# A two-block transformer on one core: the order of each engine from a simulated timeline

## The chip, the cores and the metric

The kernel runs on one core of one Trainium2 chip. The metric is the device time of the run in microseconds (us), as the median of three runs. The core's engines are TensorE (PE; its weight loads are listed as PEld), VectorE (DVE), ScalarE (ACT), GpSimd (POOL) and SyncE (SP), which here issues the DMAs of the weights. Each works off its own queue of instructions, in the order that was fixed when the program was built; they wait for one another by semaphores.

## The reference

256 tokens of width 1024 go through a first block of two layers (gated linear attention, GLA, then stick-breaking attention, SB; each followed by a squared-ReLU MLP, and each addition by a layer norm) and a second block of two layers (forgetting attention and retention side by side, a gated convolutional feed-forward net, a gated per-layer embedding), with a final rms norm. Cut to what matters here:

```python
def first_block(x, ...):
    for layer in range(DEPTH):                 # layer 0: GLA, layer 1: stick-breaking
        mix = gla_mixer(h, ...) if layer < N_A else stick_breaking_attention(q, k_sh, v_sh) @ sb_w_o[j]
        h = layer_norm(DEEPNORM_ALPHA * h + mix, ln_g[layer, 0], ln_b[layer, 0])
        h = layer_norm(DEEPNORM_ALPHA * h + sq_relu_mlp(h, mlp_w_up[layer], mlp_w_down[layer]),
                       ln_g[layer, 1], ln_b[layer, 1])

def gla_mixer(x, w_in, w_a2, b_a, norm_g, w_o):
    proj = x @ w_in                            # q, k, v, g and the low-rank gate a1
    o = gla_chunked(q, k, v, log_a)
    o = o * lax.rsqrt(jnp.mean(jnp.square(o), axis=-1, keepdims=True) + RMS_EPS) * norm_g
    return (o * jax.nn.silu(g)) @ w_o

def sq_relu_mlp(x, w_up, w_down):
    h = jax.nn.relu(x @ w_up)
    return (h * h) @ w_down
```

## The kernel before

All activations stay on the chip, features on the partitions and the 256 tokens along the row. What takes the time is the weights: some 220 MB of float32 are streamed from HBM once, in the order of the list `STREAM`. `prep` (L325 to L333) issues the DMA of half a block of weights into `raw` (128x1024, four buffers), casts it on ACT to `wh` (L330), and subtracts on DVE to get the remainder `wl` (L333); six buffers of each. Activations are split the same way by `split` (cast L467 on ACT, subtraction L468 on DVE). Every product is then three matmuls in `mm3`: wh·xh (L402), wh·xl (L403), wl·xh (L404), 128 columns of weights against 256 tokens, or 512 columns where a projection is kept with tokens on the partitions (`proj_tok`).

PSUM holds four `acc` tiles, three `up` tiles and one `aux` tile; a fourth projection into `up` has to wait until the first has been read.

At a layer norm, `layer_norm` centres the sum on an estimate of the mean and gives the un-normed, scaled input `xg`. `early` multiplies the first weight blocks of what comes next with it (matmuls of 128x258, two columns more for gain and bias). In the middle of these, `stats` sums x and its squares over the features by four fp32 matmuls (L586), L588 to L592 form mean and variance, `rsqrt` takes Ln and Exp on ACT and three steps on DVE (L501 to L503), and L597 subtracts the mean. `normed` multiplies by the reciprocal root (L618), applies gain and bias on ACT (L622) and splits (L467, L468); `settle` (L665 to L667) corrects the early products afterwards, and the MLP squares its ReLU in L712. In the second block `normed` also multiplies by an rms weight and has its own steps (L624, L626, L627, L644).

The GLA layer takes its rms norm by column sums into `aux` (L530), gates with Silu from `up` tiles (L396, behind a load of ACT's function table, L390). Stick-breaking and forgetting attention take scores (L916, L920; L1119, L1120) and multiply the weights with the values (L979, L981) into `aux`, which `split` reads for the output projection. These attention stages are called from hooks between the steps of the projections, so in program order they lie between matmuls that don't need them.

The program's order is not the order of the engines. The Tile framework gives each instruction a priority, `tc.cur_priority`, that grows along the program; `prep` adds `LATER` = 150 to that of the casts and subtractions of weights. When the context closes, a scheduler goes through the instructions and lays each engine's queue out by what is ready when, and by priority. What it takes for "ready when" is the subject of the change. Dependences without a semaphore (`add_manual_dep`) are added in a few places, as for weight casts that must not come before the end of a norm (`self.after`, the last step of `rsqrt`).

Of the kernel before, what the change touches and what calls it, by code (L numbers as in the profile page):

```python
# [1413 lines left out]
@with_exitstack  # L1414
def program(ctx: ExitStack, tc: tile.TileContext, A, out, stop=None):
    Net(ctx, tc, A, out, stop).run()


def build(inputs, stop=None):
    import concourse.bacc as bacc  # L1420

    nc = bacc.Bacc("TRN2", target_bir_lowering=False, num_devices=1)
    host, aps = {}, {}
    for name, a in arrays(inputs).items():
        host[f"in_{name}_dram"] = a
        aps[name] = nc.dram_tensor(f"in_{name}_dram", a.shape, mybir.dt.from_np(a.dtype), kind="ExternalInput").ap()
    out = nc.dram_tensor("out_0_dram", (T, D), F32, kind="ExternalOutput").ap()
    with tile.TileContext(nc) as tc:
        program(tc, aps, out, stop)
    return nc, host  # L1430

# [8 lines left out]
```

## Time and profile before

| | |
|---|---|
| time, median of 3 runs | 1300.72 us (1300.63 to 1301.56) |
| the profiled execution: its own time | 1304.21 us |
| its span | 1302.4 us |
| busy: PE, DVE, ACT | 1283.7, 950.8, 754.4 us |
| read from HBM | 227.96 MB, 177 GB/s over the span |
| mean granted clock of PE | 0.997 |

The span is the stretch of the profiled execution from the first to the last instruction. Busy time is the union of an engine's instructions, and matmuls overlap in it, so it can't be divided by their number; the distance between their starts is what one costs. "Idle before" an instruction, with the releaser behind the arrow, is a wait. Granted clock 1.00 is the upper of PE's two levels (2.4 GHz), 0.50 the lower (1.2 GHz).

### The profile page before, as it was taken

To read this page: it belongs to the slowest core of one execution; us is meant where nothing else is said; L and a number is where in the kernel's file an instruction comes from. 1 tells how busy PE (TensorE), PEld (TensorE's weight loads), DVE (VectorE), ACT (ScalarE), POOL (GpSimd) and SP (SyncE) were. 2 spreads that over 40 slices of the span, in tenths; PEclk is the share of its full clock that TensorE was granted. 3 is DMA by queue.
4 is the path that set the end of the run, shared out by engine and by line. 5 is a ranking of instruction groups with operands and counts; after the bars stand their busy time and mean duration, and the time that the engine had idled before them with its cause. 6 is when DMAs were issued, how large, how long until landed. Compare 5 with 4: busy or idle time off the path is not lost.

```text
span 1302.4 us, 25441 instructions
## 1 busy us (share of the span) xinstructions
PE 1283.7 (99%) x10302; PEld 1235.9 (95%) x10302; DVE 950.8 (73%) x1526; ACT 754.4 (58%) x1194; POOL 37.2 (3%) x89
## 2 busy tenths in 40 slices
PE   8999999999999999999999999999999999999997
PEld 6999999999899999999989999999999899999996
DVE  6989955559657955558878788765787869885855
ACT  6566744447786754446746665544674557554544
POOL 0000000000231000000000000000001000000000
PEclk9999999999999999999999999999999999999999
DMA  8655666654533576555664466565647446666561
GB/s 278 226 165 161 195 191 182 186 180 141 186 118 114 170 230 189 183 190 196 206 195 135 143 202 188 181 186 155 217 155 228 145 129 196 189 184 188 173 218 54
DMA packets 64694, 232.78 MB, mean 179 GB/s; under 512 B 7216, under 2 KB 7488, under 8 KB 63936
## 3 DMA queue, kind: packets, MB, share of 16 engines
q1 hardware_dynamic: 61920, 220.75, 54.0%
q10 hardware_dynamic: 2016, 8.28, 1.7%
q0 software_dynamic: 640, 2.11, 0.5%
q8 instruction: 81, 1.33, 0.4%
q14 instruction: 37, 0.30, 0.1%
HBM read 227.96 MB, written 3.16 MB: 177 GB/s over the span
## 4 chain that ended last, share of the span: by engine, by line
PE 88%; DVE 5%; DMA 3%; ACT 2%; issue 1%; POOL 0%; SPq 0%; POOLq 0%; DVEq 0%; ACTq 0%
PE up L402 19%; PE up L403 19%; PE up L404 19%; PE acc L403 9%; PE acc L404 8%; PE acc L402 8%; DVE wl L333 2%; DMA raw<-in_w_pg_dram 1%; PE aux L979 1%; ACT wh L330 1%; DMA wa<-in_w_a_dram 1%; PE acc L1130 1%; PE aux L586 1%; DMA raw<-in_w_gv_dram 0%; PE acc L1073 0%
## 5 line engine op out<-in xcount | busy, mean ns | idle before, releaser
L333 DVE TENSOR_TENSOR wl<-raw,wh 128x1024 fp32r<-128x1024 f32 (+2 forms) x420 | 505.3, 1207 | 257.8 <-ACT wh L330 256.2
L330 ACT CAST wh<-raw 128x1024 fp32r<-128x1024 f32 (+2 forms) x420 | 434.5, 1036 | 384.3 <-PE acc L403 141.3
L402 PE MATMUL up<-b,wh 128*128 128x256 f32 (+1 forms) x2032 | 575.0, 283 | 3.1 <-DVE pleg L1268 1.8
L403 PE MATMUL up<-b,wh 128*128 128x256 f32 (+1 forms) x2032 | 573.2, 282 | 0.9 <-DVE b L515 0.8
L404 PE MATMUL up<-b,wl 128*128 128x256 f32 (+1 forms) x2032 | 570.6, 281 | 0.0
L402 PEld LDWEIGHTS up<-b,wh 128*128 128x128 f32 x2032 | 382.2, 188 | 8.8 <-issue 3.4
L403 PEld LDWEIGHTS up<-b,wh 128*128 128x128 f32 x2032 | 383.4, 189 | 3.7 <-issue 1.6
L404 PEld LDWEIGHTS up<-b,wl 128*128 128x128 f32 x2032 | 383.6, 189 | 0.9 <-issue 0.8
L403 PE MATMUL acc<-b,wh 128*128 128x256 f32 (+1 forms) x960 | 270.6, 282 | 0.0
L404 PE MATMUL acc<-b,wl 128*128 128x256 f32 (+1 forms) x960 | 270.4, 282 | 0.0
L402 PE MATMUL acc<-b,wh 128*128 128x256 f32 (+1 forms) x960 | 270.2, 281 | 0.0
L402 PEld LDWEIGHTS acc<-b,wh 128*128 128x128 f32 x960 | 181.1, 189 | 0.1
L403 PEld LDWEIGHTS acc<-b,wh 128*128 128x128 f32 x960 | 181.0, 189 | 0.1
L404 PEld LDWEIGHTS acc<-b,wl 128*128 128x128 f32 x960 | 180.7, 188 | 0.1
L402 PE MATMUL up<-wh,b 128*128 128x512 f32 (+1 forms) x136 | 52.5, 390 | 1.6 <-ACT wh L361 1.6
L403 PE MATMUL up<-wl,b 128*128 128x512 f32 (+1 forms) x136 | 51.9, 382 | 0.0
L404 PE MATMUL up<-wh,b 128*128 128x512 f32 (+1 forms) x136 | 51.6, 381 | 0.0
L467 ACT CAST b<-ffny 128x256 fp32r<-128x256 f32 x44 | 17.9, 407 | 54.4 <-DVE ffny L1204 52.1
L402 PEld LDWEIGHTS up<-wh,b 128*128 128x128 f32 x136 | 25.5, 188 | 8.3 <-ACT wh L361 2.3
L404 PEld LDWEIGHTS up<-wh,b 128*128 128x128 f32 x136 | 25.5, 188 | 5.3
L403 PEld LDWEIGHTS up<-wl,b 128*128 128x128 f32 x136 | 25.6, 188 | 4.9 <-DVE wl L362 0.4
L1196 DVE TENSOR_TENSOR glaS<-up,rfr 128x256 f32<-128x256 f32 x44 | 18.7, 425 | 12.4 <-PE up L404 12.3
(266 smaller groups left out, 1166.2 us busy)
## 6 DMA issues: line engine op xcount, KB each, us to landing
raw<-in_w_fu_dram SPq DMA_DIRECT2D x88, 512.0 KB, 4.4
raw<-in_w_mu_dram SPq DMA_DIRECT2D x64, 512.0 KB, 4.3
raw<-in_w_md_dram SPq DMA_DIRECT2D x64, 512.0 KB, 4.6
raw<-in_w_fd_dram SPq DMA_DIRECT2D x32, 512.0 KB, 4.4
raw<-in_w_sqk_dram SPq DMA_DIRECT2D x16, 512.0 KB, 4.4
raw<-in_w_rqk_dram SPq DMA_DIRECT2D x16, 512.0 KB, 4.8
raw<-in_w_fqk_dram SPq DMA_DIRECT2D x16, 512.0 KB, 4.0
raw<-in_w_out_dram SPq DMA_DIRECT2D x16, 512.0 KB, 4.0
```

Of the source, the lines that this page charges most:

```text
L330: i = nc.scalar.copy(hi, r).ins
L333: i = nc.vector.tensor_tensor(out=lo, in0=r, in1=hi, op=ALU.subtract).ins
L402: mm(o, wh, xh, start=first, stop=False, skip_group_check=True)
L403: mm(o, wh, xl, start=False, stop=False, skip_group_check=True)
L404: self.last_mm = mm(o, wl, xh, start=False, stop=last, skip_group_check=True).ins
L467: nc.scalar.copy(out[0][:, i, :], src)
L586: nc.tensor.matmul(ps[:, k, :], ones, s[k][:, i, :], start=(k == 0 and i == 0), stop=(i == 1), skip_group_check=True)
L979: self.nc.tensor.matmul(pO[r, i // 2, :], v[:, 0, hc], ws[i][:, 0:256], start=(i < 2), stop=False, skip_group_check=True)
L1130: mm(pls[i][:, a:b], qk[r, 0, a:a + P], qk[r, 1, 0:b - a], start=(a == 0), stop=True, skip_group_check=True)
L1196: nc.vector.tensor_tensor(out=a[:, 2:], in0=ps[:, 0, :], in1=R, op=ALU.mult)
```

## The change

```diff
-    with tile.TileContext(nc) as tc:
+    with tile.TileContext(nc, schedule_with_timeline_sim=True) as tc:
         program(tc, aps, out, stop)
```

One argument is given to the context (L1428): the order of the instructions on each engine is laid out on a timeline that is simulated, in place of an estimate. Instructions, tiles, buffers and priorities in the code are the same: 10003 matmuls, the same DMAs in the same order on SP's queue. The rows of PE's order differ in 2424 lines of some 9900, DVE's in 1664 of some 1470 rows (both sides counted), ACT's in 1248 of some 1130, POOL's in 11. The orders of the two programs follow, at the places of which the prediction speaks.

PE in the GLA layer before: aux_152 is the norm's column sum, its second matmul the one that ends it; up_151 is the second block of the gate weights w_gg.

```order
L404 MATMUL up_151_872<-b8_4_88,wl_93_557 128x256
L530 MATMUL aux_152_897<-sumh_143_849,one_148 128x256
L402 MATMUL up_151_872<-b8_4_88,wh_95_562 128x256
L403 MATMUL up_151_872<-b8_5_89,wh_95_562 128x256
L404 MATMUL up_151_872<-b8_4_88,wl_96_563 128x256
L530 MATMUL aux_152_897<-suml_144_850,one_148 128x256
L402 MATMUL up_151_872<-b8_4_88,wh_95_562 128x256
```

PE there in the changed program: up_164 is the third block, up_172 the fourth, which takes the `up` slot of the first.

```order
L403 MATMUL up_164_959<-b8_5_89,wh_113_663 128x256
L530 MATMUL aux_152_897<-suml_144_850,one_148 128x256
L404 MATMUL up_164_959<-b8_4_88,wl_114_664 128x256
L402 MATMUL up_164_959<-b8_4_88,wh_113_663 128x256
L403 MATMUL up_164_959<-b8_5_89,wh_113_663 128x256
L404 MATMUL up_164_959<-b8_4_88,wl_114_664 128x256
L402 MATMUL up_172_1026<-b8_4_88,wh_128_761 128x256
```

The end of the column sum moved from the second block to the last matmuls of the third, four ahead of up_172.

PE at the entry of the first MLP before: aux_223 are the sums of x (lnsum_177) and of its squares (lnsum_178); acc_215 and acc_216 are early products of the first block of w_mu, which is at its start here.

```order
L402 MATMUL acc_216_1380<-b8_175_1082,wh_190_1147 128x258
L403 MATMUL acc_216_1380<-b8_176_1083,wh_190_1147 128x258
L404 MATMUL acc_216_1380<-b8_175_1082,wl_191_1148 128x258
L586 MATMUL aux_223_1429<-lnsum_177_1088,tab0_82 128x256 x2
L586 MATMUL aux_223_1429<-lnsum_178_1089,tab0_82 128x256 x2
L402 MATMUL acc_215_1379<-b8_175_1082,wh_190_1147 128x258
L403 MATMUL acc_215_1379<-b8_176_1083,wh_190_1147 128x258
```

PE there in the changed program; acc_229 is an early product of the second block, up_237 of the third.

```order
L402 MATMUL up_237_1527<-b8_175_1082,wh_207_1309 128x258
L403 MATMUL up_237_1527<-b8_176_1083,wh_207_1309 128x258
L586 MATMUL aux_223_1429<-lnsum_177_1088,tab0_82 128x256 x2
L403 MATMUL acc_215_1379<-b8_176_1083,wh_190_1147 128x258
...
L404 MATMUL acc_215_1379<-b8_175_1082,wl_191_1148 128x258
L402 MATMUL acc_216_1380<-b8_175_1082,wh_190_1147 128x258
L403 MATMUL acc_216_1380<-b8_176_1083,wh_190_1147 128x258
L586 MATMUL aux_223_1429<-lnsum_178_1089,tab0_82 128x256 x2
L404 MATMUL acc_216_1380<-b8_175_1082,wl_191_1148 128x258
L403 MATMUL acc_229_1465<-b8_176_1083,wh_201_1243 128x258
```

The sums stood together among the first block's early products, 108 matmuls ahead of the first one on the normed x (up_273); now early products of all three blocks stand ahead of them, the sum of the squares comes eight matmuls after the sum of x, and 51 matmuls ahead of up_273. (The second MLP's entry has the same pattern: 107 before, 30 now, with 16 matmuls between the two sums.)

DVE at the entry of the first MLP before, from the end of the reciprocal root (rfr_228, L503) to the first split of the normed x (b8_247): lnq is the normed x before gain and bias, erz the correction of early products.

```order
L503 SCALAR_TENSOR_TENSOR rfr_228_1442<-rfa_227_1441,rfr_228_1442 128x256
L666 SCALAR_TENSOR_TENSOR erz_256_1620<-spread_224_1434,erk_255_1619,acc_215_1379 128x256
L618 TENSOR_TENSOR lnq_248_1592<-b8_174_1081,rfr_228_1442 128x512
L618 TENSOR_TENSOR lnq_249_1598<-b8_174_1081,rfr_228_1442 128x512
L666 SCALAR_TENSOR_TENSOR erz_256_1620<-spread_224_1434,erk_255_1619,acc_216_1380 128x256
L666 SCALAR_TENSOR_TENSOR erz_260_1634<-spread_224_1434,erk_259_1633,acc_229_1465 128x256
L667 TENSOR_TENSOR erz_256_1620<-erz_256_1620,rfr_228_1442 128x512
L618 TENSOR_TENSOR lnq_250_1604<-b8_174_1081,rfr_228_1442 128x512
L333 TENSOR_TENSOR wl_233_1470<-raw_231_1467,wh_232_1469 128x1024
L468 TENSOR_TENSOR b8_247_1591<-b8_245_1589,b8_246_1590 128x512
```

DVE there in the changed program, from the second lnq on; lnq_248, all four L666 and the four L597 stand ahead of these rows.

```order
L618 TENSOR_TENSOR lnq_249_1598<-b8_174_1081,rfr_228_1442 128x512
L667 TENSOR_TENSOR erz_256_1620<-erz_256_1620,rfr_228_1442 128x512
L667 TENSOR_TENSOR erz_260_1634<-erz_260_1634,rfr_228_1442 128x512
L333 TENSOR_TENSOR wl_233_1470<-raw_231_1467,wh_232_1469 128x1024
L333 TENSOR_TENSOR wl_236_1476<-raw_234_1473,wh_235_1475 128x1024
L333 TENSOR_TENSOR wl_241_1532<-raw_239_1529,wh_240_1531 128x1024
L333 TENSOR_TENSOR wl_244_1538<-raw_242_1535,wh_243_1537 128x1024
L618 TENSOR_TENSOR lnq_250_1604<-b8_174_1081,rfr_228_1442 128x512
L618 TENSOR_TENSOR lnq_251_1610<-b8_174_1081,rfr_228_1442 128x512
L712 TENSOR_TENSOR relu2_257_1628<-relu_254_1618 128x512
L712 TENSOR_TENSOR relu2_261_1642<-relu_258_1632 128x512
L468 TENSOR_TENSOR b8_247_1591<-b8_245_1589,b8_246_1590 128x512 x2
```

One weight subtraction (L333) and three lnq stood between; now it is four subtractions, all four lnq and two squares of the MLP (L712), which need the early products.

PE at the entry of the stick-breaking layer before: up_525 is an early product, up_554 and up_555 the value projection (first matmuls on the normed x), acc_568 and acc_569 the first scores.

```order
L402 MATMUL up_525_3703<-b8_466_3262,wh_498_3492 128x258
L403 MATMUL up_525_3703<-b8_467_3263,wh_498_3492 128x258
L404 MATMUL up_525_3703<-b8_466_3262,wl_499_3493 128x258
L402 MATMUL up_554_3830<-wh_505_3559,b8_533_3765 128x512
L403 MATMUL up_554_3830<-wl_506_3560,b8_533_3765 128x512
...
L404 MATMUL up_555_3831<-wh_519_3644,b8_534_3766 128x512
L916 MATMUL acc_568_3889<-qk_541_3798 128x256
L916 MATMUL acc_569_3891<-qk_541_3798 128x256
L920 MATMUL acc_568_3889<-qk_541_3798 128x128
L920 MATMUL acc_569_3891<-qk_541_3798 128x128
```

PE there in the changed program; acc_594 and acc_595 are the scores of the second pair of heads.

```order
L404 MATMUL up_525_3703<-b8_466_3262,wl_499_3493 128x258
L916 MATMUL acc_568_3889<-qk_541_3798 128x256
L916 MATMUL acc_569_3891<-qk_541_3798 128x256
L920 MATMUL acc_568_3889<-qk_541_3798 128x128
L920 MATMUL acc_569_3891<-qk_541_3798 128x128
L916 MATMUL acc_594_4005<-qk_545_3810 128x256
L916 MATMUL acc_595_4007<-qk_545_3810 128x256
L920 MATMUL acc_594_4005<-qk_545_3810 128x128
L920 MATMUL acc_595_4007<-qk_545_3810 128x128
L402 MATMUL up_554_3830<-wh_505_3559,b8_533_3765 128x512
```

The scores of two pairs of heads stand in front of the value projection, where those of one stood 33 matmuls behind its start.

At the ends of the attentions (the L981 matmul into `aux`, then the split) the output projection's matmuls that read the split result now follow directly: once at w_so (up_717) and three times at w_out (up_1308, up_1911 twice); 36 matmuls or more stood between. At the second block's entry the four sums stand 26 instead of 48 matmuls ahead of the first one on the normed x.

## Rows read from the trace of the kernel before

**Rows 1.** The page: busy us (share of the span) and instructions of each engine

```profile
PE 1283.7 (99%) x10302; PEld 1235.9 (95%) x10302; DVE 950.8 (73%) x1526; ACT 754.4 (58%) x1194; POOL 37.2 (3%) x89
```

**Rows 2.** Waits of PE: waiting tile and line, releaser, sum us, times, longest

```profile
PE up L402 <- DVE pleg L1268: 1.8, 1, 1.8
PE acc L764 <- DVE wl L333: 1.7, 1, 1.7
PE up L402 <- ACT wh L361: 1.6, 1, 1.6
...
PE up L402 <- ACT b L626: 1.2, 1, 1.2
PE up L403 <- DVE b L515: 0.8, 2, 0.5
PE acc L830 <- DVE glaQ L823: 0.4, 1, 0.4
PE acc L937 <- ACT sbh L931: 0.4, 1, 0.4
PE aux L586 <- DVE lnsum L578: 0.3, 1, 0.3
```

**Rows 3.** Windows: stretch, us, busy us of five engines, PE clock, DMA share, GB/s

```profile
120.00:280.00 160.00, 160.00 (x1350) 159.92 (x1349) 101.16 (x118) 83.83 (x115) 0.00 (x0) 1.00 0.61 188
608.61:614.18 5.57, 5.57 (x26) 4.32 (x24) 5.25 (x13) 3.57 (x7) 0.00 (x0) 1.00 0.65 218
951.40:953.50 2.10, 0.31 (x3) 0.11 (x1) 2.10 (x6) 1.08 (x2) 0.00 (x0) 1.00 0.00 0
954.44:957.85 3.41, 3.41 (x18) 3.41 (x17) 2.31 (x7) 1.91 (x5) 0.00 (x0) 0.50 0.52 159
957.85:961.26 3.41, 3.41 (x31) 3.41 (x30) 3.06 (x7) 3.16 (x4) 0.00 (x0) 1.00 0.00 0
20.40:24.40 4.00, 3.89 (x20) 3.21 (x21) 4.00 (x7) 4.00 (x9) 0.00 (x0) 1.00 0.62 173
```

**Rows 4.** ACT's timeline at the GLA gates: start us, us, instruction

```profile
76.59 1.05 ACT L330 CAST wh<-raw 128x1024 fp32r<-128x1024 f32 x1 [1.49 <-PE up L403]
77.76 0.42 ACT L396 ACTIVATE rfa<-rfv 128x256 f32<-128x256 f32 x1
78.21 0.42 ACT L396 ACTIVATE rfr<-rfa 128x256 f32<-128x256 f32 x1
78.64 1.28 ACT L390 ACT_TABLE_LOAD   x1
79.94 1.09 ACT L396 ACTIVATE glaG<-up 128x512 f32<-128x512 f32 x2
```

**Rows 5.** Timelines of ACT (one row) and DVE at the first MLP's entry

```profile
120.75 0.39 ACT L588 ACTIVATE spread<-aux 128x256 f32<-128x256 f32 x1 [2.21 <-PE aux L586]
...
125.25 1.22 DVE L333 TENSOR_TENSOR wl<-raw,wh 128x1024 fp32r<-128x1024 f32 x1
126.39 0.42 DVE L503 SCALAR_TENSOR_TENSOR rfr<-rfa,rfr 128x256 f32<-128x256 f32 x1
126.72 0.47 DVE L666 SCALAR_TENSOR_TENSOR erz<-spread,erk,acc 128x256 f32<-128x256 f32 x1
127.11 1.29 DVE L618 TENSOR_TENSOR lnq<-b,rfr 128x512 f32<-128x512 f32 x2
128.32 0.86 DVE L666 SCALAR_TENSOR_TENSOR erz<-spread,erk,acc 128x256 f32<-128x256 f32 x2
129.10 0.68 DVE L667 TENSOR_TENSOR erz<-erz,rfr 128x512 f32<-128x512 f32 x1
```

**Rows 6.** Timelines: PE at the first scores; ACT and DVE at a forgetting attention's split

```profile
325.68 0.70 PE L916 MATMUL acc<-qk 64*128 64x256 f32 x4
326.22 0.39 PE L920 MATMUL acc<-qk 64*128 64x128 f32 x4
326.53 0.50 PE L402 MATMUL up<-wh,b 128*128 128x512 f32 x1
...
711.53 0.59 ACT L467 CAST b<-aux 128x512 fp32r<-128x512 f32 x1 [0.71 <-PE aux L981]
712.15 0.69 DVE L468 TENSOR_TENSOR b<-aux,b 128x512 fp32r<-128x512 f32 x1
```

## The prediction

> **What bounds the kernel now.** I read the profile in this order: busy time by engine, the waits of TensorE (PE), the stretches by windows, and then the timelines of VectorE (DVE) and ScalarE (ACT) at the places that the change touches. PE is busy for 1283.7 us, 99% of the span, DVE for 73%, ACT for 58% [rows 1]. PE's waits are few and short: the longest are 1.8, 1.7, 1.6 and 1.2 us [rows 2]. So nothing that DVE or ACT does costs time now, as long as PE has other matmuls standing in front of the one that wants the result. In the steady part 1350 matmuls take 160.00 us, 0.1185 us each at full clock [rows 3]. The order of PE's queue is therefore worth just what it hides: at every norm, and at the gates and attentions, a chain on ACT and DVE runs while PE works off matmuls that don't need it. I call these matmuls the cover of the chain.
>
> The change leaves the operations and the weight DMA queue as they are. It can gain the little idle time that is there, and it can lose cover. I went through PE's new order and counted, at each place where a chain ends in a matmul, how many matmuls stand between the one that starts the chain and the one that ends it; the chain is priced by durations of the trace of before.
>
> **Place 1, the gates of the GLA layer.** The last column sum of the norm (L530) stood some 70 matmuls ahead of the first matmul of up_172, the fourth w_gg block; now it stands 4 ahead, 0.47 us. That matmul needs the slot of up_133, which the first Silu frees (three buffers). Behind the column sum come Ln, Exp, the table load and Silu. In the trace Ln starts at 77.76 and the first of two Silus ends at about 80.5, 2.7 us later [rows 4]; DVE's mean-and-epsilon step ahead of Ln is worth about another 0.4, so 3.2 in all. The new order also puts a 1.05 us weight cast [rows 4] ahead of Ln on ACT, whose buffer only comes free at a matmul two ahead of up_172. From 3.2 − 0.5 = 2.7 to 3.2 + 1.05 = 4.2; I take **3.8**, since the cast can't start early.
>
> **Places 2 and 3, the entries of the two MLPs.** The sums for the norm (the L586 matmuls) start the chain; the first matmul on the normed x ends it. Between them stood 108 and 107 early matmuls on the un-normed input, now 51 and 30, since the L586 of the squares was moved towards the end: 51 × 0.1185 = 6.0 and 30 × 0.1185 = 3.6 us of cover instead of 12.8. On DVE the new order puts 26 instructions ahead of the split (L468) that gives the first x its low half. Four weight subtractions (L333), two L712 and six L666/L667, which stood partly behind, are now among them. Prices, by the distance from one start to the next [rows 5]: 13 of 128x512 at 1.21 / 2 = 0.61 are 7.9; 4 of L333 at 126.39 − 125.25 = 1.14 are 4.6; 6 of 128x256 at 0.39 are 2.3; L501 to L503 at 0.42 are 1.3; while Ln and Exp run, DVE has to wait for 0.9 (77.76 to 78.64 on ACT [rows 4]); ahead of it all stands ACT's L588, 0.39 [rows 5]. The sum is 17.4 us. Less the cover that is **11.4** at MLP 0 and **13.8** at MLP 1. The low bound is a DVE that has done the four subtractions before the sums arrive and idles during Ln anyway: −4.6 + 0.9, 7.7 and 10.1. The order of each engine is fixed, though, and these four stand behind L503, so I stay near the top.
>
> **Place 4, the stick-breaking attention.** The cover is 79 early matmuls, 9.4 us, but the scores of the first two head pairs (L916, L920), which stood 33 matmuls behind the first w_sv matmul, now stand in front of it. They need DVE's and ACT's settle of the early projections, and themselves take 0.85 us for four (eight rows, 325.68 to 326.53) [rows 6], 1.7 for both; two 512-wide matmuls more, 0.23 each by 5.57 us for 24 [rows 3], go before the low half of x is asked for. Cover: 11.6. DVE's run has 11 of 128x512 (6.7), 6 of 128x256 (2.3), five L333 (5.7), 1.3, 0.9 and 0.4: 17.3. Late by **5.7** (4 to 6, the low end if the scores' wait and DVE's run end together).
>
> **Place 5, the entry of the second block.** The sums moved 22 matmuls down: 48 matmuls of cover, 24 × 0.1185 + 24 × 0.23 = 8.4, became 26, some 5.8 us. PE already waits 1.2 here [rows 2], so the high half comes 2.6 later, and the low half a further 2.0, as two half-size L333 and four L624 now stand ahead of L627: **4.6** (2 to 5.5).
>
> **Place 6, attention output straight into its projection, four times** (once w_so, three times w_out). Before, 36 or more matmuls of other heads stood behind the last L981 matmul. Now the projection that reads its result stands right behind it, and must wait for cast (0.59) and subtraction (0.69) [rows 6]: 1.3 each, **5.2** in all. From 2.5, if the cast alone counts, to 8, if one of ACT's weight casts (1.05) is in front of the cast two or three times.
>
> Sum of the losses: 3.8 + 11.4 + 13.8 + 5.7 + 4.6 + 5.2 = 44.5.
>
> **The clock.** In the trace of before it fell once: after PE had been idle for 1.8 us [rows 2, 3], the granted clock of the stretch that follows is 0.50 (the 1.2 GHz level) for 3.41 us, in which 18 matmuls were done where the next 3.41 us hold 31 [rows 3]: 13 × 0.1185 = 1.5 us lost. After the idle of 1.7 us at L764 it was 1.00 [rows 3]. The new idles are 4 to 14 us long at five places. Nothing in this trace shows idles of that length. I take one such fall behind each of the five: 7.5, less the old fall if its idle shrinks, 1.5: **+6.0** (0 if none follows, 17 if each lasts twice as long). The Trainium skill, "TensorE: Matmul & The Clock Gate", section "Part 1: The HAM clock gate", says that "the default state is throttled, and activity releases the throttle". By that rule each of the five long idles would be followed by a slow stretch, the +6.0 above; the one fall in the trace agrees with it, and the 1.7 us idle with none shows that a short idle doesn't always do it.
>
> **Gains.** The waits at L764 (1.7), L830 (0.4), L937 (0.4) and L586 (0.3) [rows 2] lie where the new order has other matmuls in front, and the two at the embedding gate (1.8 and 0.5) shrink to about 1.2, a gain of 1.1 to 1.4: **−4.2** (−2 to −5.4, all but the kernel's start).
>
> **Sum.** 44.5 + 6.0 − 4.2 = **+46.3**. The profiled execution took 1304.21 us (span 1302.4), 3.5 above the median of the timed runs; the difference is added to the median: 1300.72 + 46.3 = **1347**. Low ends added up, 2.7 + 7.7 + 10.1 + 4 + 2 + 2.5 + 0 − 5.4 = 23.6, give 1324; high ends 4.2 + 11.4 + 13.8 + 6 + 5.5 + 8 + 17 − 2 = 63.9, give 1365.
>
> **Rivals.** (a) *Only the MLP entries cost much.* DVE idles 27% of the span [rows 1], enters each run with nothing left over, and the subtractions and splits overlap with waits that I count apart. The MLP entries at their low ends, 17.8, half of the other places, 10, clock +3 and gains −4.2: 26.6, **1327**. Against it: the new order has the subtractions and squares inside the chain, behind L503, so an idle DVE can't do them early. Chance 0.15, at 1318 to 1335.
> (b) *The clock stays low.* If each of some ten new idles over 1 us is followed by slow stretches of twice 3.41 us, they cost 30 rather than 6: about **1371**. For: one of two idles of about the same length did it [rows 3]; against: full clock was back after 3.41 us. Chance 0.11, from 1362.
> (c) *Faster.* At MLP 0 DVE's run would have to fit under the 6.0 us of cover, and so on at each place; then only the gains are left: −5.4 and −1.5 of the old clock fall, **1294**. It decides itself at DVE's run: 17.4 us against 6.0 and 3.6; even without the four subtractions it is 12.8. It would need the norm's 128x512 instructions to run in under a third of their 0.61 us, or to be behind L468, where they are not. Chance 0.03.
> (d) *The change doesn't do what it says:* the moved rows are such as were ready long before, and PE finds each of them ready: 1300.7. Against it stand the counts of cover, which are far shorter than the chains. Chance 0.02.
>
> **How the numbers follow.** Forecast 1347, from 1335 to 1362: 0.69. The rivals get 0.15, 0.11, 0.03 and 0.02. The range holds 8 in 10 with half of (a) and a part of (b): **1326 to 1364**. A measurement of this kernel tells about 0.2% (2.6 us) from no change; faster by more 0.03, within 0.02, slower 0.95.
>
> **What would show it.** In the profile of after, PE's waits should list, in this order of size: the first normed matmul of MLP 1 and of MLP 0 (L402 and L403, released by ACT L467 and DVE L468, together 14 and 11 us), L916 and the w_sv matmul (6), the second block's first normed matmul (L402/L403, 4 to 6), up_172 behind Silu (4), four of 1 to 3 us behind L467/L468 after L981; DVE's timeline should show 26 instructions without a gap at the MLP entries; the windows behind the long idles should show 0.50 of the clock for about 3.4 us. Wrong would be: MLP waits under 5 us (then the run of DVE was ahead), or a total beyond the sum of the listed waits by more than 10 us (then the clock did it).

## The result, and the profile after

The changed kernel takes **1361.62 us** (1360.85 to 1363.03, 4 runs) against 1301.14 us (1300.63 to 1302.65): the ratio is 1.0462 (95% interval 1.0449 to 1.0474), 60.5 us slower. 1347 was forecast, with a range of 1326 to 1364. The sign, the places and the sizes of the large waits came out as worked out. One kind of loss was not in the sum at all, and the clock cost more than it held; the waits as a whole cost less, so that the errors partly cancel, and the sum lay some 14 us too low.

The busy times and the clock by slices of the page, after (the row for the busy times before is [rows 1]):

```profile
PE 1310.4 (96%) x10302; PEld 1252.1 (92%) x10302; DVE 953.1 (70%) x1526; ACT 756.0 (56%) x1194; POOL 39.3 (3%) x89
...
PEclk9989799999999989999899999999999999999999
```

DVE and ACT do the same work in nearly the same time (950.8 and 754.4 us before); PE's busy time has grown by 27 us, though it runs the same 10302 rows. Two things make a matmul longer in such a row: the lower clock, which shows as an 8 or a 7 in four of the slices, and what stands next to it in the queue.

PE's waits, after (waiting tile and line, releaser, sum in us, times, longest; [rows 2] before):

```profile
PE up L402 <- ACT b L467: 21.2, 6, 10.4
PE up L403 <- DVE b L468: 6.4, 3, 3.0
PE acc L916 <- ACT qk L897: 4.0, 1, 4.0
PE up L402 <- ACT glaG L396: 3.7, 1, 3.7
PE up L402 <- ACT b L626: 2.9, 1, 2.9
PE up L403 <- DVE b L627: 1.8, 1, 1.8
...
```

These six rows hold the six places of the prediction (L467 and L468 stand for places 2, 3 and 6, L626 and L627 for place 5); below them stand 1.2 us and less. Two timelines of after show the largest, the entries of the two MLPs (start in us, length, instruction, idle before it and releaser), PE at the first and then at the second, and then DVE and two rows of ACT at the first:

```profile
137.33 0.28 PE L404 MATMUL up<-b,wl 128*128 128x258 f32 x1
145.48 0.58 PE L402 MATMUL up<-b,wh 128*128 128x256 f32 x1 [7.87 <-ACT b L467]
149.09 0.58 PE L403 MATMUL up<-b,wh 128*128 128x256 f32 x1 [3.02 <-DVE b L468]
...
468.38 0.28 PE L404 MATMUL up<-b,wl 128*128 128x258 f32 x1
479.05 0.58 PE L402 MATMUL up<-b,wh 128*128 128x256 f32 x1 [10.39 <-ACT b L467]
482.66 0.58 PE L403 MATMUL up<-b,wh 128*128 128x256 f32 x1 [3.03 <-DVE b L468]
```

```profile
131.94 2.50 DVE L597 TENSOR_TENSOR b<-b,spread 128x512 f32<-128x512 f32 x4 [3.90 <-ACT spread L588]
...
140.20 1.29 DVE L667 TENSOR_TENSOR erz<-erz,rfr 128x512 f32<-128x512 f32 x2
141.40 4.62 DVE L333 TENSOR_TENSOR wl<-raw,wh 128x1024 fp32r<-128x1024 f32 x4
145.94 1.29 DVE L618 TENSOR_TENSOR lnq<-b,rfr 128x512 f32<-128x512 f32 x2
147.15 1.29 DVE L712 TENSOR_TENSOR relu<-relu 128x512 f32<-128x512 f32 x2
148.35 1.29 DVE L468 TENSOR_TENSOR b<-b,b 128x512 fp32r<-128x512 f32 x2
...
137.48 3.87 ACT L330 CAST wh<-raw 128x1024 fp32r<-128x1024 f32 x4
...
144.83 1.12 ACT L467 CAST b<-b 128x512 fp32r<-128x512 f32 x2
```

From the last early matmul to the L403 that wants the low half of x, PE runs one matmul in 11.8 us at the first MLP and in 14.3 at the second. DVE goes through its 26 instructions with no gap but the one for Ln and Exp, and the four weight subtractions take 4.62 us in the middle of them, as the order said. PE's first wait there ends with ACT's cast L467, behind four weight casts of 3.87 us, and its second with DVE's run.

To see the rest, I took the starts of PE's 10302 rows in each trace and sorted the distances from each to the next into three: those over 0.6 us (waits), the excess over 0.1195 us of the shorter ones where the granted clock is 0.50 (clock), and all else.

| us | waits | clock | all else | sum |
|---|---|---|---|---|
| before | 12.4 | 1.5 | 1279.3 | 1293.2 |
| after | 46.9 | 12.4 | 1293.0 | 1352.3 |
| difference | +34.5 | +10.9 | +13.7 | +59.1 |

The prediction had +40.3 for waits (44.5 less 4.2), +6.0 for the clock, and nothing for the third column. One part of that column is no matmul's place in the queue: at the start of the kernel nine matmuls of 512 columns stand 0.43 us apart in after (7.24 to 10.66), as such matmuls do in its low stretch at 344, where in the trace of before most stand 0.23 apart. The clock record of after begins only at 10.82, so 1.5 us of the 13.7 are most likely clock. It doesn't come from the change: the first matmuls stand 0.43 apart in most traces here, those of the old order too (six in b_kst18 and in b_upone6). The experiments take the three columns apart.

### The profile page after: what moved, and what is told of

Same layout as the page of the kernel before. It is cut to its first block, busy times and chain, and to the rows that moved or that the text cites. A ratio compares the mean times of both kernels' runs of the same rounds, so it can differ in the third digit from the quotient of the medians.

```text
span 1361.3 us, 25482 instructions
## 1 busy us (share of the span) xinstructions
PE 1310.4 (96%) x10302; PEld 1252.1 (92%) x10302; DVE 953.1 (70%) x1526; ACT 756.0 (56%) x1194; POOL 39.3 (3%) x89
## 4 chain that ended last, share of the span: by engine, by line
PE 93%; DVE 4%; ACT 2%; issue 1%; DMA 0%; POOLq 0%; SPq 0%; DVEq 0%; POOL 0%
PE up L403 20%; PE up L402 20%; PE up L404 20%; PE acc L402 9%; PE acc L403 9%; PE acc L404 9%; PE aux L979 1%; DVE wl L333 1%; PE acc L1130 1%; PE aux L586 1%; ACT wh L330 1%; PE aux L981 0%; PE acc L1073 0%; PE acc L916 0%; DVE b L597 0%
## 5 line engine op out<-in xcount | busy, mean ns | idle before, releaser
L333 DVE TENSOR_TENSOR wl<-raw,wh 128x1024 fp32r<-128x1024 f32 (+2 forms) x420 | 506.1, 1209 | 278.6 <-ACT wh L330 277.9
L402 PE MATMUL up<-b,wh 128*128 128x256 f32 (+1 forms) x2032 | 574.5, 285 | 27.8 <-ACT b L467 21.2
L403 PE MATMUL up<-b,wh 128*128 128x256 f32 (+1 forms) x2032 | 577.3, 285 | 8.9 <-DVE b L468 6.4
L402 PEld LDWEIGHTS up<-b,wh 128*128 128x128 f32 x2032 | 385.3, 191 | 34.9 <-ACT b L467 22.6
L403 PEld LDWEIGHTS up<-b,wh 128*128 128x128 f32 x2032 | 386.5, 190 | 14.7 <-DVE b L468 8.1
L403 PE MATMUL acc<-b,wh 128*128 128x256 f32 (+1 forms) x960 | 270.0, 282 | 0.0
L402 PE MATMUL acc<-b,wh 128*128 128x256 f32 (+1 forms) x960 | 267.4, 282 | 0.0
L403 PEld LDWEIGHTS acc<-b,wh 128*128 128x128 f32 x960 | 180.9, 189 | 0.2
L402 PEld LDWEIGHTS acc<-b,wh 128*128 128x128 f32 x960 | 179.2, 188 | 0.1
L402 PE MATMUL up<-wh,b 128*128 128x512 f32 (+1 forms) x136 | 52.9, 397 | 1.2 <-ACT wh L361 1.2
L403 PE MATMUL up<-wl,b 128*128 128x512 f32 (+1 forms) x136 | 53.3, 392 | 0.0
L402 PEld LDWEIGHTS up<-wh,b 128*128 128x128 f32 x136 | 26.2, 194 | 7.1 <-ACT wh L361 1.9
L403 PEld LDWEIGHTS up<-wl,b 128*128 128x128 f32 x136 | 26.4, 194 | 6.0 <-DVE wl L333 0.4
L1200 ACT ACTIVATE ffny<-glaS,vec 128x256 f32<-128x256 f32 x44 | 25.7, 598 | 0.0
```

Source lines behind the costliest of these rows:

```text
L333: i = nc.vector.tensor_tensor(out=lo, in0=r, in1=hi, op=ALU.subtract).ins
L402: mm(o, wh, xh, start=first, stop=False, skip_group_check=True)
L403: mm(o, wh, xl, start=False, stop=False, skip_group_check=True)
L1200: nc.scalar.activation(y, a[:, 2:], AF.Identity, scale=self.col(f"cw{l}2", f), bias=self.col(f"cb{l}", f))
```

## Experiments

### The waits: late sums alone, and the chain they start

Is it the cover, or DVE's and ACT's order, that makes 11 to 14 us of wait at the MLP entries? **b_kst18** is the kernel before with one constant changed, so that the norm's sums come late, and nothing else:

```diff
-KST, KSS, KPL, KRM, KSP = 5, 5, 1, 7, 3
+KST, KSS, KPL, KRM, KSP = 18, 5, 1, 7, 3
```

> The kernel before, with one constant changed, so that the norm's sums at the two MLP entries stand 30 matmuls ahead of the first normed one, as in the changed kernel at the second MLP (108 before); everything else is ordered as before. On DVE only 18 instructions stand between, none of them a weight subtraction, and on ACT two weight casts of which one is behind Exp. If cover alone decides (the prediction's step): 11 to 14 of wait at each entry and the clock as in the changed kernel, 1328 to 1334. Theory A with the chain as it stands in this order: 8 of 128x512 at 0.61, 6 of 128x256 at 0.39, 1.3, 0.9 and 0.4 are 9.8 us, less 3.6 of cover 6.2 at each entry, and 1.5 to 3 of clock behind each: 1314 to 1320.

It took 1315.93 us against 1301.21 (ratio 1.0111, 1.0095 to 1.0127), as the chain in this order said. PE's largest wait there, and the two low stretches behind the entries (stretch, us, busy us of the engines, PE clock, DMA share, GB/s):

```profile
PE up L402 <- ACT b L467: 10.2, 2, 5.2
```

```profile
136.07:142.90 6.83, 5.56 (x24) 5.27 (x25) 6.83 (x11) 6.80 (x17) 0.00 (x0) 0.50 0.13 31
446.68:453.51 6.83, 5.42 (x23) 5.13 (x24) 6.83 (x11) 6.83 (x17) 0.00 (x0) 0.50 0.09 21
```

With 30 matmuls of cover and the old order on DVE and ACT the waits are 5.0 and 5.2 us at L402, and some 0.6 more at L403 by the distance of starts (0.73 less a step). In after, with 51 and 30, they are 10.9 and 13.4. So the second entry, where the cover is the same, owes 7.6 of its 13.4 us to what stands inside the chain. On DVE these are eight instructions more: four subtractions (4 × 1.14 = 4.6) and four of 128x512 (L618, L667 and two L712, 4 × 0.61 = 2.4); on ACT there are four weight casts in place of two. The two causes don't split cleanly. In the kernel before 12.8 us of cover stood against a chain of 9.8, so that late sums alone cost 5.6 and 5.8, but they cost more where the chain is longer.

**e2_pin** goes the other way, from the changed kernel: the sums are put back to where they were among the early matmuls, at the two MLP entries and at the stick-breaking entry.

```diff
             for o in range(2):
-                self.mm3(ps[o], *w(k * 2 + o), xg[0][:, k, :], xg[1][:, k, :], k == 0, k == KB - 1)
+                with self.tc.issue_after(ln["sum"]) if k + step > kst else nullcontext(): self.mm3(ps[o], *w(k * 2 + o), xg[0][:, k, :], xg[1][:, k, :], k == 0, k == KB - 1)
...
-                    nc.tensor.matmul(ps[:, k, :], ones, s[k][:, i, :], start=(k == 0 and i == 0), stop=(i == 1), skip_group_check=True)
+                    ln["sum"] = nc.tensor.matmul(ps[:, k, :], ones, s[k][:, i, :], start=(k == 0 and i == 0), stop=(i == 1), skip_group_check=True).ins
```

> The changed kernel, with PE's early matmuls that follow the norm's sums in the program held behind these sums at the two MLP entries and the stick-breaking entry, so that the cover is again some 108 matmuls (12.8 us); DVE's and ACT's order stays nearly that of the changed kernel. Theory A: the chain of 17.4 us against 12.8 leaves 4.6 at each MLP in place of 11.5 and 14, and the idles are too short for a long low stretch, so 16 of waits and 5 to 8 of clock come back, less what the sums now wait for their own inputs (L578, L579 on DVE, 2 to 5 in all): 1340 to 1347. If the cover were not what decides, but DVE's and ACT's order: 1355 to 1362.

1348.38 us (1.0358, 1.0343 to 1.0374): 13.2 less than after, at the small end of what was expected and 1.4 us beyond it. Waits fell from 46.9 to 35.3 us: the distances to the first normed matmuls at the MLP entries from 26.0 to 7.7, and the wait at L916 from 4.0 to 0.9. New ones came up in front of the sums (distances of starts, L586 at the first MLP 2.3 and 0.6; L403 and L586 at the second 1.2, 2.3 and 1.1), since DVE's new order also makes the sums' inputs later than before; I had 2 to 5 for these, they are 7.5. The clock column did not fall (12.5): five low stretches again, two of them at places that e2_pin doesn't touch.

### The clock: fill the idles

**e1_fill** leaves the waits and takes away the idleness: matmuls whose results nobody reads run while PE waits.

```diff
     def mm3(self, o, wh, wl, xh, xl, first, last):
         mm = self.nc.tensor.matmul
-        mm(o, wh, xh, start=first, stop=False, skip_group_check=True)
-        mm(o, wh, xl, start=False, stop=False, skip_group_check=True)
+        pre(self); mid(self, mm(o, wh, xh, start=first, stop=False, skip_group_check=True).ins)
+        post(self, mm(o, wh, xl, start=False, stop=False, skip_group_check=True).ins)
...
+FILL = {0: (66, 26), 1: (88, 26), "g": (28, 0), "m": (44, 32)}
...
+def pad(self, n, behind):
+    src = self.want[2]
+    for _ in range(n):
+        i = self.nc.tensor.matmul(self.pz[:, 0:min(T, src.shape[1])], src[:, 0:P], src[:, 0:min(T, src.shape[1])], start=True, stop=True, skip_group_check=True).ins
+        for b in behind:
+            self.tc.add_manual_dep(i, b.name, NOSYNC, reason="pad")
+        behind = [i]
+    return behind
```

> The changed kernel, with extra matmuls (results unused) put into PE's long idles at four places: 28 ahead of up_172 at the GLA gates, 66 ahead of the first normed matmul and 26 between its L402 and L403 at the first MLP, 88 and 26 at the second, 44 and 32 of half width at the second block's entry. Each block is a little shorter than the idle it fills, so the waits for ACT and DVE end when they did; what changes is that PE isn't idle. Theory A (of the 60.5 us lost, some 34 are waits, some 11 to 12 the low clock behind them, and the rest comes from PE's attention matmuls standing in smaller pieces): the four low stretches vanish, and with them the half speed of the matmuls that really ran in them, worked out from the changed kernel's trace as 3.4 + 2.5 + 3.0 + 1.9 = 10.8: 1351, and the stretch behind the stick-breaking entry, which is not filled, stays low. Theory B (all that is not in the listed waits is the clock, 44 us of low stretches at half speed): 22 less, 1340. If the low clock had another cause than the idle in front of it: 1361 to 1362, and the low stretches stay.

1357.67 us (1.0426, 1.0408 to 1.0443), only 4 less, but the traces tell why. The low stretches of after, one behind each of the five long idles:

```profile
85.91:92.74 6.83, 5.64 (x26) 5.65 (x27) 5.33 (x14) 3.76 (x9) 0.00 (x0) 0.50 0.24 77
140.52:154.17 13.65, 5.66 (x25) 5.37 (x26) 13.51 (x20) 10.60 (x23) 0.00 (x0) 0.50 0.46 154
338.50:345.33 6.83, 5.19 (x21) 4.37 (x22) 6.80 (x11) 6.23 (x17) 0.00 (x0) 0.50 0.76 235
471.62:488.69 17.07, 6.61 (x29) 6.32 (x30) 15.90 (x24) 14.00 (x27) 0.00 (x0) 0.50 0.39 123
666.18:673.01 6.83, 4.69 (x20) 4.40 (x21) 6.83 (x18) 5.15 (x12) 0.00 (x0) 0.50 0.82 283
```

The stretches of e1_fill that hold the four filled places:

```profile
82.00:92.00 10.00, 9.88 (x81) 9.51 (x81) 8.73 (x17) 6.84 (x13) 0.00 (x0) 1.00 0.56 159
133.00:153.00 20.00, 19.91 (x165) 19.52 (x163) 18.96 (x32) 15.35 (x29) 0.00 (x0) 1.00 0.33 106
460.00:485.00 25.00, 24.91 (x204) 24.53 (x204) 21.59 (x36) 16.50 (x35) 0.00 (x0) 1.00 0.32 102
655.00:675.00 20.00, 20.00 (x163) 19.45 (x162) 16.86 (x39) 12.16 (x26) 0.00 (x0) 1.00 0.62 209
```

All four are at 1.00, and the one place that was not filled stays low behind its idle of 4.0 us (6.83 us at 0.50 from 337.24 on). So the idle is the cause of the fall. The chain is as long as before: from the last early matmul to the first L402 it is 8.15 us in after and 8.17 in e1_fill at the first MLP, 10.67 and 10.69 at the second, 3.97 and 3.98 at the gates. The clock column went from 12.4 to 3.8, 8.6 us of gain against 10.8 expected. Of these, 3.3 were given back by my own filling at the second block's entry, where the half-width matmuls took as long as the full ones and the two distances grew from 3.25 and 2.26 to 5.09 and 3.69; the rest is smaller waits at other places (1.1 behind the stick-breaking scores, 0.8 at the start). Theory B, by which 22 us of the loss were clock, falls.

The Trainium skill, "TensorE: Matmul & The Clock Gate", section "Part 1: The HAM clock gate", has it that the default is throttled and activity releases it. The traces agree: each of the five idles (2.9 us at the second block's entry, 10.4 at the second MLP) has its low stretch, and none has one once it is filled. The one low stretch of the kernel before lasted 3.41 us [rows 3]; here they last 6.83 to 17.07 us, the two longest where PE waits another 3.0 us inside the stretch.

### The third column: matmul groups cut into pieces

Where the third column's 13.7 us are can be seen where an attention group ends, in after (PE, start and length, a row for several matmuls of one kind):

```profile
374.01 0.28 PE L404 MATMUL up<-b,wl 128*128 128x256 f32 x1
374.23 1.08 PE L979 MATMUL aux<-sbw,b 128*64 128x256 f32 x6
375.23 0.39 PE L402 MATMUL up<-b,wh 128*128 128x256 f32 x1
375.46 0.28 PE L403 MATMUL up<-b,wh 128*128 128x256 f32 x1
375.67 0.43 PE L979 MATMUL aux<-sbw,b 128*64 128x256 f32 x1
...
376.68 0.38 PE L404 MATMUL up<-b,wl 128*128 128x256 f32 x1
```

Eight L979 and eight L981 rows (four matmuls of each in the program) are cut once, with two projection matmuls between, and take 376.68 − 374.23 = 2.45 us with these. In **e4_row** the eight matmuls of a group are chained in the queue, the one whose input is ready last coming first; before there were 12 such groups, after 30 pieces, here again 12:

```diff
-            for i in range(4):
+            for i in (3, 2, 1, 0):
...
-                    self.nc.tensor.matmul(pO[r, i // 2, :], v[:, 0, hc], ws[i][:, 0:256], start=(i < 2), stop=False, skip_group_check=True)
+                    row(self, 3 - i, self.nc.tensor.matmul(pO[r, i // 2, :], v[:, 0, hc], ws[i][:, 0:256], start=(i > 1), stop=False, skip_group_check=True).ins)
...
+def row(self, n, i):
+    if n:
+        self.tc.add_manual_dep(i, self.one_mm.name, NOSYNC, reason="row")
+    self.one_mm = i
```

> The changed kernel, with the eight matmuls L979 and L981 of each head group held together, as they stood before (12 groups; in the changed kernel 30 pieces with projection matmuls between). The places of the waits stay. Theory A: where a single L979 stands between projection matmuls, the next projection matmul starts 0.31 after it instead of 0.12, and the L979 are no longer pairwise at 0.10; from the distances of starts in the two traces the pieces of L979 and L981 cost about 7 us: 1354 to 1356. If such pieces cost nothing (theory B): 1361 to 1363.

1351.22 us (1.0381, 1.0364 to 1.0399): 10.4 less than after, more than the 5 to 7 I expected. The same group in its trace:

```profile
373.17 1.08 PE L979 MATMUL aux<-sbw,b 128*64 128x256 f32 x8
374.09 0.61 PE L981 MATMUL aux<-sbw,b 128*64 128x128 f32 x8
374.62 0.39 PE L403 MATMUL up<-b,wh 128*128 128x256 f32 x1
```

1.45 us for the 16 rows in one piece; the cut one took 2.45 − 2 × 0.12 = 2.21, so one cut cost 0.76. Over the program the third column falls from 1293.0 to 1280.2, all but 0.9 of what it had grown by, while the waits grow by 3.8, since a group in one piece begins later. Both traces have the slow start. "Pieces" is thus nearly all of that column.

One part of the change alone says the same. **b_cut** is the kernel before with its four stick-breaking groups set apart and nothing else:

```diff
-            hk += [(K2, lambda: s2(j - 2, 0)), (K22, lambda: s2(j - 2, 1)), (K3, lambda: s3(j - 2))]
+            hk += [(K2, lambda: s2(j - 2, 0)), (K22, lambda: s2(j - 2, 1))] + [(K3 - 3 + q, lambda q=q: s3(j - 2, q)) for q in range(4) if j % 2]
...
-    self.split(o, slice(j - 1, j + 1), self.pv(v, 2 * (j - 1) * 64, ws[j - 1] + ws[j]))
+    cut(self, v, 2 * (j - 1) * 64, ws[j - 1] + ws[j], q) or self.split(o, slice(j - 1, j + 1), self.pO)
```

> The kernel before, with one thing of the change alone: in the stick-breaking attention the four L979 of each of its four head groups are set apart, 6 to 13 projection matmuls between them, as the changed kernel has them; 12 pieces more, no wait added (the last L979 and all L981 stand where they were). If pieces cost what e4_row says (10.4 us for 18 pieces, 0.58 each, part of which may be the clock): 12 times 0.45 to 0.6 = 5.4 to 7, 1306.5 to 1308.5. If the gain of e4_row came from anything else than the pieces: 1300.5 to 1302.

1308.43 us (1.0051, 1.0038 to 1.0065), 6.4 more than before: 0.53 for each of the 12 pieces. Its third column stands 6.6 above before. A lone L979 in its trace (L1450 is L979 there; two rows are one matmul of the program):

```profile
344.98 0.28 PE L404 MATMUL up<-b,wl 128*128 128x256 f32 x1
345.19 0.65 PE L1450 MATMUL aux<-sbw,b 128*64 128x256 f32 x2
345.76 0.39 PE L402 MATMUL up<-b,wh 128*128 128x256 f32 x1
345.99 0.28 PE L403 MATMUL up<-b,wh 128*128 128x256 f32 x1
```

The L979 starts 0.21 after the projection matmul in place of 0.12, the next projection matmul 0.57 after that, where in the row of eight two rows take 0.92 / 4 = 0.23, and the one behind it 0.23 in place of 0.12: 0.09 + 0.34 + 0.11 = 0.54 for a piece. An L979 is 64 columns wide (128*64). The Trainium skill, "TensorE: Matmul & The Clock Gate", section "Part 3: Packing small matmuls — row/col tiling", says that matmuls on different tiles of the array run side by side. The trace agrees: in the group of eight the rows start in pairs, 0.01 us apart, with 0.21 to 0.26 from pair to pair. The two rows of a lone L979 start 0.27 apart, so a pair is made of two heads, and a lone one has nothing to run beside.

### Do the three add up, and what the priorities were worth

**e7_all** joins e2_pin and e4_row, and moves the four casts and subtractions at the MLP entries behind the norm's last split:

```diff
+            cast() if self.after is None or self.put is None else self.put.append(cast)
...
+def flush(self):
+    put, self.put = self.put, None
+    for cast in put or ():
+        for i, j in zip(cast(), self.first):
+            self.tc.add_manual_dep(i, j.name, NOSYNC, reason="put")
```

> The changed kernel with three things put back at once: the norm's sums ahead of the early matmuls (as in e2_pin), the L979 and L981 groups in one piece (as in e4_row), and at the MLP entries the four weight casts and subtractions, which stand inside the chain of the norm, moved behind its last split. If cover, chain and pieces are separate causes, the gains of e2_pin (13.2) and e4_row (10.4) add, and of the 7.6 us that still wait for the first normed matmuls in e2_pin (1.4, 3.5 and 2.7) some 3 to 6 go, since ACT's four casts are 3.9 and DVE's four subtractions 4.6: 1361.6 - 13.2 - 10.4 - 3 to 6 = 1332 to 1335. If they overlap (one cause seen twice): 1340 to 1348.

1334.06 us (1.0249, 1.0235 to 1.0263), as the sum of the parts said: 13.2 and 10.4, and 4.0 for the third, by which the distances to the first normed matmuls at the MLP entries shrink from e2_pin (1.4, 3.5 and 2.7, here 0.6, 1.5 and 1.5). The third part was not run by itself. L467 as a releaser of PE is down to 3.8 us. Beside it stand places that e7_all doesn't touch (L396, L626), and waits in front of the sums that the pinning itself made (L570):

```profile
PE up L402 <- ACT b L467: 3.8, 5, 1.3
PE up L402 <- ACT glaG L396: 3.7, 1, 3.7
PE acc L403 <- DVE b L570: 3.0, 2, 2.0
PE up L402 <- ACT b L626: 2.9, 1, 2.9
```

Of the 32 us that still lie between this and the kernel before, the columns give 19.6 to waits, 10.6 to the clock (some 1.9 of it the slow start, which is on record in this trace) and 1.4 to all else.

In the changed program `LATER`, the constant that holds the weight casts back, does next to nothing: with 600 for 150 the order of every engine is the same, row for row. With it and `LATER_PG` at 0, 8 matmuls, 3 instructions on DVE and 5 on ACT stand elsewhere; in the kernel before the same zeros move 172, 210 and 118 (counted in the orders of the programs; the changed kernel was not run so). **b_later0** takes both out of the kernel before:

```diff
-LATER = 150
-LATER_PG = [80, 80, 80, 0]
+LATER = 0
+LATER_PG = [0, 0, 0, 0]
```

> The kernel before, scheduled by the estimate as before, but with LATER and LATER_PG at 0, so that the casts and subtractions of weights have the priority of their place in the program. In the changed kernel these constants don't act at all: with LATER at 600 its order is the same on every engine, row for row. This asks how much of the 60.5 us is their loss. At the two MLP entries the cover is 88 and 79 matmuls here (10.4 and 9.4 us), and DVE has 5 L333 in the run to the first L468: 6 of 128x512 at 0.61, 5 at 1.14, 6 of 128x256 at 0.39, 1.3 and 0.4 are 13.4, with the wait for Ln and Exp up to 14.3. That leaves 3 to 4 of wait at the first and 4 to 5 at the second, and 1.5 to 3 of clock behind each; no attention group is cut (12 groups of L979 and L981): 1311 to 1317. If the priorities were most of the loss: 1335 or more; if they are worth nothing: 1301 to 1303.

1331.26 us (1.0222, 1.0205 to 1.0239), 14 more than the high end I gave. The MLP entries came out near what was counted (3.2 and 5.9 us by the distances of starts, for 3 to 4 and 4 to 5), but I had looked at these alone. Weight casts also get in the way elsewhere: of the 3.5 us behind L515, 2.65 stand at one matmul (961.17), and DVE runs two weight subtractions ahead of the L515 that releases it:

```profile
PE up L402 <- ACT b L467: 5.4, 3, 2.7
PE up L403 <- DVE b L515: 3.5, 2, 2.6
...
```

```profile
957.76 1.23 DVE L333 TENSOR_TENSOR wl<-raw,wh 128x1024 fp32r<-128x1024 f32 x1 [0.40 <-ACT wh L330]
...
959.50 1.22 DVE L333 TENSOR_TENSOR wl<-raw,wh 128x1024 fp32r<-128x1024 f32 x1
960.63 0.48 DVE L515 SCALAR_TENSOR_TENSOR b<-b,vec,b 128x256 fp32r<-128x256 f32 x1
```

Its columns stand 13.2, 9.8 and 6.4 above before. The third grows here although all 12 groups are whole; what it is there stays open, so a rise of that column is not by itself a sign of cut groups. Without these offsets the old scheduler's order thus loses some 30 us too. That this is half of the 60.5 is not shown: the two orders lose at partly different places. Why the simulated timeline puts the sums late and cuts the groups, no run shows.

### A faster one

The kernel before has one fall of the clock, behind 1.8 us of idle at the embedding gate [rows 2, 3]. **b_upone6** removes that idle:

```diff
-        rps = [self.proj(f"w_rg{l}", c, x, hooks=((KRM, stat),) if c == 0 else ((KSP, over),)) for c in range(2)]
+        rps = both([self.proj_part(f"w_rg{l}", c, x, 8, ((7, stat),) if c == 0 else ((7, over),), 6) for c in range(2)])
...
-            for os in (((0, 1),) if c < 3 else ((0,), (1,))):
+            for os in ((0, 1),):
...
+def both(parts):
+    for _, rest in parts:
+        rest()
+    return [p for p, _ in parts]
```

> An attempt at a faster kernel from what the traces show of the kernel before: its one fall of the clock stands behind an idle of 1.8 us at the embedding gate, where the last half block has to wait for DVE's reading of the other half of the same tile (L1268). Here the last block is computed whole, and the two projections that follow (w_rg) are begun with six of their eight steps each before the last two, so that what waits for the last features has 36 matmuls more as cover. No idle over 1 us should be left there, and no fall of the clock behind it: 1.8 + 0.8 + 1.5 = 4.1 less, 1297; at least 1.5 to 2 if the wait only moves: 1299. If idles of this size cost nothing in the end: 1301.

1299.79 us against 1302.02 in the same runs: 0.9983 (0.9974 to 0.9991), 2.2 us faster than the kernel before, and the fastest here, but less than the 4.1 expected. The waits at the gate are gone and no stretch is low in the clock record from 10.19 us to PE's last matmul, but L830, which waited 0.4 [rows 2], waits 1.5. **b_bundle** adds a later place for the gate matmuls L764:

```diff
-            pv = self.proj_tok("w_gv", j, x, hooks=[(11, rank), (14, gates)] if j == 0 else ())
+            pv = self.proj_tok("w_gv", j, x, hooks=[(11, rank)] if j == 0 else [(1, gates)])
```

> b_upone6 with a second move: the gate matmuls L764, for which PE idles 1.7 us in the kernel before, stand six projection matmuls (1.4 us) later. The idle should shrink to 0.3, and L830 waits up to 0.5 longer, since the gates' chain starts later: 0.5 to 1.2 less than b_upone6, 1295.5 to 1296.5. If the wait reappears at L830 in full: the same as b_upone6.

1303.67 us (1.0008, 0.9999 to 1.0017), 3.9 more than b_upone6, where 0.5 to 1.2 less was expected: the gain is lost again. In the trace of b_upone6 PE hardly waits for L764's input (0.2 us, for 1.7 in the trace of before), so there was nothing left to hide, and the later gates make L830 wait longer. The first row of b_bundle's waits; a low stretch of 3.41 us stands behind it:

```profile
PE acc L830 <- DVE glaQ L823: 2.7, 1, 2.7
```

## Why the prediction was right, and where not

- **What bounds the kernel**: right. PE has the same rows to run, and whatever it loses it loses by order. But the sentence that the change "can gain the little idle time that is there, and it can lose cover" took the time of a matmul as independent of its neighbours. That is the step that failed; e4_row puts 12.8 us of the third column down to it. The order showed the cut groups, and I read them for waits only.
- **Place 1**: 3.8 was worked out, 3.7 is the row.
- **Places 2 and 3**: 11.4 and 13.8; measured from start to start, less two steps, 11.5 and 14.0. DVE's run, which ends last, is the one that was counted. But the larger wait of each entry, at L402, ends with ACT's cast behind its four weight casts, and ACT's run was not priced. b_kst18 and e7_all show that what stands inside the chain matters beside the cover: 7.6 of 13.4 us at the second entry, and 4.0 at the two entries when the four casts and subtractions are moved.
- **Place 4**: 5.7; the wait at L916 is 4.0, and no wait is left for the low half of x. The low clock behind the first wait slowed PE (the scores' 16 rows took 2.9 us, 340.14 to 343.07, for the 1.7 priced), and DVE was done by then.
- **Place 5**: 4.6 more than before; the distances to L402 and L403 are 3.25 and 2.26 against one of 1.56, so some 3.8 more.
- **Place 6**: 5.2; the distances over 0.6 us behind these splits (0.95, 0.95, 1.19 and 0.61, 0.95) are 4.65, less what five steps take, 4.05.
- **Gains**: 4.2 were taken off. The distances over 0.6 us that are gone add up to 8.6, or 7.8 less seven steps: the wait at the embedding gate is gone and not only shorter, and so is that at L486 (1.3), which the sum left out. Not all of it is the new order's doing: the 1.7 us at L764 are also absent from the waits of b_kst18, which has the old order there. That wait comes and goes between executions; on what it hangs is not shown.
- **The clock**: five falls, as counted, but 10.9 in place of 6.0. The size of one fall was mis-sized: the trace of before had a stretch of 3.41 us, after an idle of 1.8; behind idles of 2.9 to 10.4 us they are two to five times as long. The high end of 17 doesn't follow from its own words: five falls of twice the length are 15, less the old 1.5. Rival (b) had the length right for three of the five and the number of idles too high.
- **Rivals** (a), (c) and (d) fall: none of the chains was overlapped away, and no old wait was worth as much as one of the new.

The kernel is 60.5 us slower, and its waits grew by 34.5. That is the prediction's own second sign of being wrong (a total over 10 us beyond the waits), for which it named the clock as the cause; the clock is 10.9 of the difference, and the cut groups are as large a part. That the result lies in the range is in part luck: the waits were set 5.8 too high and the clock 4.9 too low, and the term that was missing took up the room that the high ends of the clock and of place 6 had left.

## What to carry to other kernels

In a kernel with one engine at 99%, an order is worth the matmuls that stand between the start of a chain and its end, and how little else stands inside the chain on the engines that run it: count both, at each chain. Count also the places where matmuls of another shape are set singly among full ones, 0.5 to 0.8 us each here, since they show as busy time and in no list of waits. And before a tuned kernel is laid out by another scheduler, see whether its priorities still act there: a constant that moves hardly a row of the order is the sign that they don't.

## What the runs showed of the hardware

A matmul of 64 columns (two rows in the trace) took 0.23 us in a group of four and cost 0.54 more when it stood alone among full-width ones. Behind idles of 2.9 to 10.4 us PE ran at 1.2 GHz for 6.83 to 17.07 us, and not at all so when unread matmuls filled the idle. Unread matmuls of 128 columns took 0.11 us each, hardly less than those of 256 at 0.12, so the half width filled twice the time that I had meant it to.
